# Strassen halves of an FFN cut inside each half of the tokens, a two-pass output projection and earlier fetches for the down products

## The chip, the cores and the metric

The kernel runs on one core of a Trainium2 chip. What counts is the device time of one launch in microseconds (us), as the median of several executions. A core has five engines that work side by side, each with its own queue of instructions: TensorE (PE, matrix products into PSUM), VectorE (DVE), ScalarE (ACT), GpSimd (POOL) and SyncE (SP, which here issues the DMAs). An instruction waits at the head of its queue until its operands and its buffer are there, and all that is queued behind it on that engine waits too.

## The reference, cut to what matters

Two layers work on 1032 tokens (1024 of a prompt, 8 of a sample group) with 1024 features each. Everything is float32.

```python
for l in range(DEPTH):                                    # DEPTH = 2
    main, mo = mixer(l, rmsnorm(x, norm_mix_g[l]))        # layer 0: RG-LRU, layer 1: windowed attention
    x = x + concat([main, mo]) @ w_out[l]                 # output projection, 1024 x 1024
    hn = rmsnorm(x, norm_ffn_g[l])
    u = hn @ w_ffn_up[l]                                  # 1024 x 6144: gates, values
    u = causal_dwconv(u, width=3) + bias
    x = x + (gelu(u[:, :3072]) * u[:, 3072:]) @ w_ffn_down[l]
```

The change touches three stages of each layer: the output projection, the up products and the start of the down products. The mixers stay as they are.

## The kernel before, in words

Features lie on the 128 partitions, tokens on the free axis. Nearly all data live in one pool of 44 row buffers of 128 x 1032 numbers (`row()`); small ones of 392 columns come from a pool of 12 (`sm()`), and products go to 8 PSUM buffers of 512 columns (`ps()`).

A product keeps float32 accuracy by splitting each operand into a high part (a rounded copy, made by ACT at L108) and a low part (the operand less the high part, a subtraction by DVE at L116 or by POOL at L119). `mm3` then makes three matmuls of each pair of tiles: L301 (high by high), L302 (high by low) and L303 (low by high). Helpers record most vector instructions, so one line stands for many: L108 is every activation or copy of ACT, L116 `vtt` and L122 `stt` on DVE (the second also scales by a gain), L119 `gtt` on POOL.

**Output projection** (`out_proj`). The tokens are cut into four quarters of 258 (QW). The eight output blocks are worked through in passes (layer 0: blocks 0 to 3, then 4 to 7; layer 1: 0 and 1, 2 and 3, then 4 to 7); within a pass it goes quarter by quarter, and in each quarter block by block. A tile is 24 matmuls of 258 columns; DVE then adds its PSUM to the residual `x[m]`. A weight is fetched and split once, and held through its pass. After each quarter of the last pass `on_block` starts the norm of this quarter.

**Norm and operands** (`enter_ffn`). `norm(q)` stores the quarter of the residual to DRAM (`rD`), squares and sums it, multiplies the sums by a matrix of ones on PE (L580), and scales the eight blocks with eight instructions on DVE (L122). The up products follow Strassen's scheme in Winograd's form: gates and values of block pair j, the two halves of the features, and the two halves of the tokens (columns 0 to 515 and 516 to 1031) make the 2 x 2 blocks. Seven products P1 to P7 stand for eight. Their token operands B11, B21, B22 and the differences T1 to T4 (28 tiles of 516 columns with a high and a low part each) are made once per layer. B22 and T1 to T4 need quarters 2 and 3 of the tokens, so they come after the last quarter's norm.

**Up products** (`ffn`). There are 24 pairs. Each product's weights are combined on POOL and split (copy by ACT, low part by POOL, 512 columns each) five products ahead (AHEAD). A product is 24 matmuls of 258 columns in two column halves, each in a PSUM buffer of its own. Pairs 0 and 1 are interleaved product by product (`ENTRY`); from pair 2 on the order is `STEADY`. After a pair, `post` runs the convolution (one activation, two taps on DVE at L122, an add for the sample tokens), gelu and the product, and stores the gated block to DRAM (`gD`, L883).

**Down products.** The 24 gated blocks are read in four chunks of six. For chunk 0 six blocks are loaded (L953) and split on ACT and DVE, then the eight tiles of the residual are loaded again from `rD` (L979), and the first weight of `w_ffn_down` is asked for (L254). A tile of the residual takes three PSUM buffers (384, 384 and 264 columns) per chunk.

**What sets the order.** ACT follows the order in which the program is written. The other engines' queues are ordered by the framework's scheduler, which weighs its own estimates of when operands are ready. SP's queue holds all these DMAs; a load waits there until a row buffer is free, a store until its data is ready. `get` fetches and splits weights in the order of one list (`spec_...`), one ahead; a fence keeps the down weights from being asked for before the first `get` of one.

## Time and profile before

| | |
|---|---|
| median of 3 runs | 2588.8 us (2584.58 to 2590.01) |
| the profiled execution, its own time | 2590.59 us |
| its span | 2588.8 us |
| busy share of the span | PE 90%, DVE 60%, POOL 53%, ACT 41% |
| mean granted clock of PE | 0.951 of full speed |

The span is what the profiler saw from first to last instruction; 1.8 us of the execution's time lie around it. A slice of the page's picture is a fortieth of the span, 64.7 us, and a digit is the busy share of the slice in tenths. Layer 0's output projection ends in the 8th slice, its up products in the 16th; for layer 1 these are the 28th and the 36th.

### The profile page before, as it was taken

How to read it: one execution, taken by the hardware profiler on the slowest of the kernel's cores; microseconds unless marked ns; L12 is line 12 of the kernel's file. 1: busy time of each engine (PE TensorE's matmuls, PEld its weight loads, DVE VectorE, ACT ScalarE, POOL GpSimd, SP SyncE). 2: the span in 40 equal slices, each digit the busy share in tenths (PEclk: the TensorE clock that was granted, in tenths of full speed). 3: DMA queues.
4: the chain of work that ended last, by engine and by line, in shares of the span. 5: the costliest groups of instructions: out<-in, count | busy, mean ns of one | idle time of the engine just before them, and what ended most of it. 6: DMA issues, size and time to landing. Idle time of an engine off the chain costs nothing.

```text
span 2588.8 us, 42624 instructions
## 1 busy us (share of the span) xinstructions
PE 2327.0 (90%) x16590; PEld 2247.7 (87%) x16590; DVE 1560.5 (60%) x2786; ACT 1050.6 (41%) x2181; POOL 1384.2 (53%) x1083
## 2 busy tenths in 40 slices
PE   7996888499999995999989987794999999959999
PEld 6886788399999995999977877794999999959999
DVE  6759974756666664332478789737566666643221
ACT  5665552344343443111365577513443434431110
POOL 2247651578888882222144456325788888822120
PEclk8998989799999997999989999897999999979999
DMA  4221151022222215322574543630222222153221
GB/s 163 90 68 46 51 179 59 2 74 74 83 89 76 74 58 212 109 88 76 177 265 132 181 169 118 175 130 5 74 74 81 84 82 75 58 210 105 92 73 65
DMA packets 140186, 265.24 MB, mean 102 GB/s; under 512 B 28288, under 2 KB 85200, under 8 KB 139984
## 3 DMA queue, kind: packets, MB, share of 16 engines
q1 hardware_dynamic: 139984, 262.52, 29.8%
q8 instruction: 130, 2.13, 0.3%
q14 instruction: 72, 0.59, 0.1%
HBM read 203.60 MB, written 58.87 MB: 101 GB/s over the span
## 4 chain that ended last, share of the span: by engine, by line
PE 67%; DVE 8%; issue 6%; POOL 3%; ACT 3%; DMA 3%; SPq 0%; POOLq 0%; DVEq 0%; ACTq 0%
PE ps L301 21%; PE ps L302 21%; PE ps L303 21%; POOL row L119 3%; ACT row L108 2%; DVE row L116 2%; DVE row L122 1%; DVE sm L116 1%; DMA row<-in_w_ffn_down 1%; DVE ty L116 1%; DVE ty L398 1%; DMA row<-rD 1%; ACT sm L108 0%; DMA row<-mD 0%; DVE row L1140 0%
## 5 line engine op out<-in xcount | busy, mean ns | idle before, releaser
L301 PE MATMUL ps<-row,row 128*128 128x258 f32 (+4 forms) x5032 | 1500.4, 302 | 109.9 <-ACT row L108 107.0
L119 POOL TENSOR_TENSOR row<-row,row 128x512 fp32r<-128x512 f32 (+10 forms) x714 | 1127.5, 1602 | 833.6 <-ACT row L108 447.8
L302 PE MATMUL ps<-row,row 128*128 128x258 f32 (+4 forms) x5032 | 1503.0, 301 | 32.1 <-DVE row L116 27.9
L303 PE MATMUL ps<-row,row 128*128 128x258 f32 (+4 forms) x5032 | 1471.2, 300 | 9.3 <-POOL row L119 9.3
L301 PEld LDWEIGHTS ps<-row,row 128*128 128x128 f32 x5032 | 956.9, 191 | 128.0 <-ACT row L108 116.7
L302 PEld LDWEIGHTS ps<-row,row 128*128 128x128 f32 x5032 | 960.8, 191 | 48.4 <-DVE row L116 32.8
L303 PEld LDWEIGHTS ps<-row,row 128*128 128x128 f32 x5032 | 944.5, 191 | 18.2 <-POOL row L119 10.7
L108 ACT ACTIVATE row<-row 128x512 fp32r<-128x512 f32 (+8 forms) x684 | 469.5, 723 | 987.4 <-POOL row L119 281.7
L116 DVE TENSOR_TENSOR row<-row,ps 128x258 f32<-128x258 f32 (+2 forms) x736 | 322.3, 445 | 746.8 <-PE ps L303 735.2
L122 DVE SCALAR_TENSOR_TENSOR row<-row,fw,row 128x1023 f32<-128x1023 f32 x192 | 272.1, 1436 | 64.2 <-ACT row L108 63.9
L116 DVE TENSOR_TENSOR row<-row,row 128x1032 f32<-128x1032 f32 (+8 forms) x220 | 222.0, 1027 | 56.8 <-ACT row L108 46.7
L108 ACT ACTIVATE row<-ps 128x258 f32<-128x258 f32 (+6 forms) x430 | 157.7, 407 | 97.6 <-PE ps L303 47.8
L119 POOL TENSOR_TENSOR row<-row,ty 128x768 f32<-128x768 f32 (+2 forms) x56 | 77.1, 1378 | 158.6 <-DVE ty L415 65.4
L108 ACT ACTIVATE row<-row,fw 128x1032 f32<-128x1032 f32 x96 | 114.9, 1244 | 66.1 <-DVE row L116 66.1
L116 DVE TENSOR_TENSOR row<-row,sb 128x8 f32<-128x8 f32 x96 | 105.5, 1099 | 0.0
L108 ACT ACTIVATE sm<-row 128x258 f32<-128x258 f32 (+3 forms) x130 | 51.1, 450 | 112.9 <-DVE row L122 57.9
L108 ACT ACTIVATE row<-ps,ty,ty 128x256 f32<-128x256 f32 (+1 forms) x160 | 87.5, 564 | 7.9 <-DVE ty L116 5.7
L116 DVE TENSOR_TENSOR sm<-sm,sm 128x258 f32<-128x258 f32 (+5 forms) x125 | 75.9, 616 | 19.6 <-ACT sm L108 15.9
L108 ACT ACTIVATE sm<-ps 128x384 f32<-128x384 f32 (+5 forms) x156 | 65.3, 445 | 38.3 <-PE ps L433 22.7
L116 DVE TENSOR_TENSOR row<-ps,row 128x384 fp32r<-128x384 f32 (+2 forms) x125 | 63.5, 519 | 23.2 <-ACT row L108 9.9
L119 POOL TENSOR_TENSOR row<-row 128x512 f32<-128x512 f32 x48 | 62.9, 1311 | 23.5 <-DMA rD<-row 16.1
L119 POOL TENSOR_TENSOR sm<-sm,row 128x192 f32<-128x192 f32 (+3 forms) x72 | 49.3, 698 | 36.1 <-ACT sm L108 18.6
(162 smaller groups left out, 1488.0 us busy)
## 6 DMA issues: line engine op xcount, KB each, us to landing
row<-in_w_ffn_up SPq DMA_DIRECT2D x96, 512.0 KB, 3.2
gD<-row SPq DMA_DIRECT2D x48, 516.0 KB, 2.6
row<-gD SPq DMA_DIRECT2D x48, 516.0 KB, 4.1
row<-in_w_ffn_down SPq DMA_DIRECT2D x64, 384.0 KB, 3.1
row<-hD SPq DMA_DIRECT2D x48, 512.0 KB, 6.5
rD<-row SPq DMA_DIRECT2D x64, 129.0 KB, 2.5
row<-rD SPq DMA_DIRECT2D x16, 516.0 KB, 9.9
row<-in_w_out SPq DMA_DIRECT2D x16, 512.0 KB, 4.7
```

Of the source, the lines that this page charges most:

```text
L108: return nc.scalar.activation(out, in_, func, **kw)
L116: return V.tensor_tensor(out=out, in0=a, in1=b, op=op)
L119: return G.tensor_tensor(out=out, in0=a, in1=b, op=op)
L122: return V.scalar_tensor_tensor(out=out, in0=a, scalar=s, in1=b, op0=op0, op1=op1)
L301: T.matmul(out, ah, bh, start=first and j == 0, stop=False, skip_group_check=more)
L302: T.matmul(out, ah, bl, start=False, stop=False, skip_group_check=more)
L303: T.matmul(out, al, bh, start=False, stop=last and j == n - 1, skip_group_check=more)
L398: V.tensor_reduce(out=mx[:, c0 : c0 + m], in_=s3, axis=AX.X, op=amax, negate=True)
```

## The change

**Strassen halves inside each token half.** Token half 0 is quarters 0 and 1, half 1 is quarters 2 and 3. The columns of a 2 x 2 scheme are now the two quarters of one half, so that each half has its own operands B11 to T4, with 258 columns each, in the same buffers. A product is the same 24 matmuls, 12 for each token half, with one PSUM buffer per half, and the result goes to the same places of the gates and values.

**Projection in two passes.** `out_proj` goes through all eight blocks for token half 0, then again for half 1; the weights stand twice in the list, so each is fetched and split twice. `on_tile` stores a quarter tile of the residual and squares and sums it as soon as it is added. `on_half` makes both sums' inverse roots (matmul with ones, now at L1334 of the new kernel) and starts the operands of this half. Norm and operands of half 0 and the seven combined weights of pair 0 (`first_pair`) are written beside the second pass. Pair 0 then runs first for half 0, then for half 1; pair 1 is no longer interleaved with it.

**Fetches in the last pair.** While the seven products of the last pair are issued, `fetch` loads gated blocks 0 to 5, `gated` splits blocks 0 to 4, and the first two down weights are asked for. The residual's tiles come two ahead of the tile in which they are needed (`refill`), and the blocks of the next chunk two before they are split.

Lines that only move, and removed lines that the code above shows, are left out:

```diff
 STEADY = ("P1", "P6", "P2", "P7", "P5", "P4", "P3")
-ENTRY = (
-    (0, "P1"), (1, "P1"), (0, "P2"), (1, "P2"), (0, "P6"), (1, "P6"), (0, "P7"), (1, "P7"), (0, "P4"), (1, "P4"),
-    (0, "P5"), (0, "P3"), (1, "P5"), (1, "P3"),
-)
-SEQUENCE = ENTRY + tuple((j, p) for j in range(2, KF) for p in STEADY)
+ENTRY = tuple((0, p, (0,)) for p in STEADY) + tuple((0, p, (1,)) for p in ("P1", "P2", "P6", "P7", "P5", "P4", "P3"))
+SEQUENCE = ENTRY + tuple((j, p, (0, 1)) for j in range(1, KF) for p in STEADY)
...
     def spec_out(l):
+        for hb in range(2):
+            for m in range(KD):
+                spec(f"out{l}.{hb}.{m}", I["w_out"][l, m, 0], (8, P))
...
+    def out_proj(l, mget, ks, x, on_tile, on_half):
+        for hb in range(2):
+            for m in range(KD):
+                key = f"out{l}.{hb}.{m}"
+                wh, wl = get(key, 1, 1)
+                if x[m] is None:
+                    x[m] = residual(l, m)
+                for q in (2 * hb, 2 * hb + 1):
+                    c0 = QB[q]
                     p = ps()
                     mm3(p[:, :QW], [(wh[:, k * P : k * P + P], wl[:, k * P : k * P + P]) + mget(k, c0, QW) for k in ks])
                     vtt(x[m][:, c0 : c0 + QW], x[m][:, c0 : c0 + QW], p[:, :QW], add)
+                    on_tile(q, m)
                     tick()
+                drop(key)
+            on_half(hb)
...
             if name == "P1":
-                load_pair(j + 1)
+                if j:
+                    load_pair(j + 1)
...
+        def product(j, name, hfs):
+            w = made[j, name]
+            if hfs[-1] == 1:
+                del made[j, name]
             group = {"P1": "X", "P2": "X", "P6": "Y", "P7": "Y", "P4": "Y", "P5": "Z", "P3": "Z"}[name]
             fresh = name in ("P1", "P6", "P5")
             B = PRODUCTS[name]
+            for hf in hfs:
+                if fresh:
+                    bank[j, group, hf] = ps()
                 terms = []
                 for kk in range(4):
+                    need(B, kk, hf)
+                    terms.append((w[:, kk * P : kk * P + P], w[:, 512 + kk * P : 512 + kk * P + P]) + ops[B, kk, hf])
+                mm3(bank[j, group, hf][:, :QW], terms, fresh, True, not fresh)
...
+        gh, gl, ga = {}, {}, {}
+        def fetch(j):
+            ga[j] = row()
+            SY.dma_start(ga[j][:, :NT], gD[l, j])
...
+        def refill(m):
+            x[m] = row()
+            SY.dma_start(x[m][:, :NT], rD[l, m])
         last = []
-        for q, (j, name) in enumerate(SEQUENCE):
-            while at < min(len(SEQUENCE), q + AHEAD):
-                combine(*SEQUENCE[at])
+        todo = [(0, p) for p in STEADY] + [(j, p) for j, p, _ in SEQUENCE if j]
+        at = 7
+        for q, (j, name, hfs) in enumerate(SEQUENCE):
+            if q == 6:
+                load_pair(1)
+            want = 7 if q < 10 else min(len(todo), q - 7 + AHEAD)
+            while at < want:
+                combine(*todo[at])
                 at += 1
-            t = product(j, name)
+            if j == KF - 1:
+                i = STEADY.index(name)
+                if i < DCH:
+                    fetch(i)
+                if i > 1:
+                    gated(i - 2)
+                if i == 4:
+                    get(f"dn{l}.0.0", 0, 1)
         def down(c, m, b):
...
-        for j in range(DCH):
+        for j in range(5, DCH):
             gated(j)
-            tick()
+        refill(0)
+        refill(1)
         for t in last:
             finish(t)
         SY.dma_start(O[4][l], ul)
-        for m in range(KD):
-            x[m] = row()
-            SY.dma_start(x[m][:, :NT], rD[l, m])
         for c in range(NDC - 1):
             for m in range(KD):
-                if m >= 2:
+                if c == 0 and m + 2 < KD:
+                    refill(m + 2)
+                if m < DCH:
+                    fetch((c + 1) * DCH + m)
+                if m > 1:
...
     def enter_ffn(l, x, mh, ml):
+        ops, gen, sums = {}, {}, {}
+        def split(name, kk, hf, pair, raw, on_pool):
             hi, lo = pair
             acopy(hi, raw)
             (gtt if on_pool else vtt)(lo, raw, f(hi), sub)
+            ops[name, kk, hf] = pair
+        def cols(q):
+            return slice(QB[q], QB[q] + QW)
+        def on_tile(q, m):
+            SY.dma_start(rD[l, m, :, cols(q)], x[m][:, cols(q)])
+            if m == 0:
+                sums[q] = sm()
+                act(sums[q][:, :QW], x[m][:, cols(q)], AF.Square)
+            else:
+                t = sm()
+                act(t[:, :QW], x[m][:, cols(q)], AF.Square)
+                vtt(sums[q][:, :QW], sums[q][:, :QW], t[:, :QW], add)
+        def inverse(q):
+            a = sums.pop(q)
+            p = ps()
+            T.matmul(p[:, :QW], ones, a[:, :QW], start=True, stop=True)
+            m, out, t = sm()[:, :QW], sm()[:, :QW], sm()[:, :QW]
+            ts(V, m, p[:, :QW], 1.0 / D, EPS, mul, add)
+            act(out, m, AF.Ln)
+            act(out, out, AF.Exp, scale=-0.5)
+            stt(t, m, -0.5, out, mul, mul)
+            vtt(t, t, out, mul)
+            stt(out, t, 1.5, out, add, mul)
+            return out
+        def norm(hf):
+            qa, qb = cols(2 * hf), cols(2 * hf + 1)
+            ra, rb = inverse(2 * hf), inverse(2 * hf + 1)
+            yield
+            xs = lambda k, part: x[k][:, part]
+            def scale(k, part, r):
+                stt(xs(k, part), xs(k, part), g_ffn[l][k], r, mul, mul)
+            def slot(k, part):
+                return mh[k][:, part], ml[k][:, part]
+            def own(n):
+                for i in range(n):
+                    if i % 2 == 0:
+                        t = row(F32R)
+                    b = (i % 2) * 2 * QW
+                    yield t[:, b : b + QW], t[:, b + QW : b + 2 * QW]
             for k in range(KD):
+                scale(k, qa, ra)
+                split("B11" if k < 4 else "B21", k % 4, hf, slot(k, qa), xs(k, qa), k % 2)
+                if k % 4 == 3:
                     yield
...
+            t2 = own(4)
+            for kk in range(4):
+                scale(kk, qb, rb)
+                scale(kk + 4, qb, rb)
+                vtt(xs(kk, qa), xs(kk, qb), xs(kk, qa), sub)
+                vtt(xs(kk, qb), xs(kk + 4, qb), xs(kk, qb), sub)
+                split("B22", kk, hf, slot(kk + 4, qb), xs(kk + 4, qb), True)
+                vtt(xs(kk + 4, qb), xs(kk + 4, qb), xs(kk, qa), sub)
+                split("T2", kk, hf, next(t2), xs(kk + 4, qb), False)
+                if kk % 2:
                     yield
+            t2 = own(4)
+            for kk in range(4):
+                split("T3", kk, hf, next(t2), xs(kk, qb), kk % 2)
+            yield
+            for kk in range(4):
+                split("T1", kk, hf, slot(kk, qb), xs(kk, qa), kk % 2)
+                if hf:
                     x[kk] = None
+            yield
+            t2 = own(4)
+            for kk in range(4):
+                vtt(xs(kk + 4, qa), xs(kk + 4, qa), xs(kk + 4, qb), sub)
+                split("T4", kk, hf, next(t2), xs(kk + 4, qa), kk % 2)
+                if hf:
                     x[kk + 4] = None
+            yield
+        weights = up_weights(l)
+        def first_pair():
+            weights[0](0)
+            yield
+            yield
+            yield
+            for name in STEADY:
+                weights[1](0, name)
+                yield
+        def on_half(hf):
+            if hf:
+                finish(gen["w"])
+            gen[hf] = start(norm(hf))
+            if not hf:
+                gen["w"] = spawn(first_pair())
+        def need(name, kk, hf):
+            while (name, kk, hf) not in ops:
+                advance(gen[hf])
+        return on_tile, on_half, need, ops, weights
...
```

**First place: SP's queue from the last up products of layer 0 to its first down products.** gD are the stored gated blocks, rD the stored residual, ul a small output. Of the kernel before, then of the changed one:

```order
L953 DMA row_10369<-gD 128x1032
L979 DMA row_10376<-rD 128x1032
L979 DMA row_10378<-rD 128x1032
L979 DMA row_10380<-rD 128x1032
L979 DMA row_10382<-rD 128x1032
L979 DMA row_10384<-rD 128x1032
L979 DMA row_10386<-rD 128x1032
L979 DMA row_10388<-rD 128x1032
L979 DMA row_10390<-rD 128x1032
L254 DMA row_10392<-in_w_ffn_down 128x768
L254 DMA row_10398<-in_w_ffn_down 128x768
```

```order
L941 DMA row_10274<-gD 128x1032
L941 DMA row_10310<-gD 128x1032
L941 DMA row_10342<-gD 128x1032
L888 DMA gD<-row_10229 128x1032
L941 DMA row_10374<-gD 128x1032
L941 DMA row_10408<-gD 128x1032
L251 DMA row_10414<-in_w_ffn_down 128x768
L251 DMA row_10420<-in_w_ffn_down 128x768
L941 DMA row_10448<-gD 128x1032
L995 DMA out<-ul 128x480
L951 DMA row_10497<-rD 128x1032
L951 DMA row_10499<-rD 128x1032
```

Before, the last two of the six gated blocks and the eight residual tiles stood ahead of the first down weight; now the gated blocks come first, weights 1 and 2 behind the fifth of them, and the residual after them, two tiles at first.

**Second place: DVE near the end of layer 0's output projection.** An add with ps is the residual add of a tile; an instruction with pack scales by the gain; sm are sums and roots of the norm. Before, then after:

```order
L122 SCALAR_TENSOR_TENSOR sm_4262<-sm_4498,sm_4262 128x258
L116 TENSOR_TENSOR row_4043<-row_4043,ps_4472 128x258
L116 TENSOR_TENSOR sm_4425<-sm_4425,sm_4504 128x258
L122 SCALAR_TENSOR_TENSOR row_3489<-row_3489,pack,sm_4262 128x258
L122 SCALAR_TENSOR_TENSOR row_3530<-row_3530,pack,sm_4262 128x258
L122 SCALAR_TENSOR_TENSOR row_3573<-row_3573,pack,sm_4262 128x258
L122 SCALAR_TENSOR_TENSOR row_3611<-row_3611,pack,sm_4262 128x258
L122 SCALAR_TENSOR_TENSOR row_3977<-row_3977,pack,sm_4262 128x258
L122 SCALAR_TENSOR_TENSOR row_4011<-row_4011,pack,sm_4262 128x258
L122 SCALAR_TENSOR_TENSOR row_4043<-row_4043,pack,sm_4262 128x258
L122 SCALAR_TENSOR_TENSOR row_4071<-row_4071,pack,sm_4262 128x258
L116 TENSOR_TENSOR sm_4425<-sm_4425,sm_4507 128x258
L116 TENSOR_TENSOR row_4071<-row_4071,ps_4510 128x258
```

```order
L119 SCALAR_TENSOR_TENSOR sm_4068<-sm_4069,sm_4068 128x258
L119 SCALAR_TENSOR_TENSOR row_3489<-row_3489,pack,sm_4068 128x258
L119 SCALAR_TENSOR_TENSOR row_3595<-row_3595,pack,sm_4068 128x258
L119 SCALAR_TENSOR_TENSOR sm_4081<-sm_4079,sm_4080 128x258
L119 SCALAR_TENSOR_TENSOR row_3663<-row_3663,pack,sm_4068 128x258
L119 SCALAR_TENSOR_TENSOR row_3731<-row_3731,pack,sm_4068 128x258
L119 SCALAR_TENSOR_TENSOR row_3799<-row_3799,pack,sm_4068 128x258
L119 SCALAR_TENSOR_TENSOR row_3867<-row_3867,pack,sm_4068 128x258
L119 SCALAR_TENSOR_TENSOR row_3935<-row_3935,pack,sm_4068 128x258
L119 SCALAR_TENSOR_TENSOR row_4003<-row_4003,pack,sm_4068 128x258
L113 TENSOR_TENSOR sm_4081<-sm_4081,sm_4080 128x258
L113 TENSOR_TENSOR row_3489<-row_3489,ps_4094 128x258
```

Before, these were the scalings of one quarter and the adds of the last tiles. Now this is the start of the second pass, and the add of its first tile (row_3489 with ps_4094) stands behind the root and the scalings of half 0.

**Third place: PE at the end of layer 0's output projection.** ps_4510 before is the PSUM of the projection's last tile, L301 to L303 are the three matmuls of `mm3` (L298 to L300 in the changed kernel). Before, then after:

```order
L303 MATMUL ps_4510<-row_3475,row_4040 128x258
L301 MATMUL ps_4510<-row_3479,row_4039 128x258
L302 MATMUL ps_4510<-row_3480,row_4039 128x258
L303 MATMUL ps_4510<-row_3479,row_4040 128x258
L301 MATMUL ps_4573<-row_3459,row_4551 128x258
L301 MATMUL ps_4574<-row_3459,row_4551 128x258
L301 MATMUL ps_4642<-row_3459,row_4558 128x258
L301 MATMUL ps_4643<-row_3459,row_4558 128x258
L302 MATMUL ps_4573<-row_3460,row_4551 128x258
L303 MATMUL ps_4573<-row_3459,row_4551 128x258
```

```order
L298 MATMUL ps_4700<-row_3479,row_4606 128x258
L299 MATMUL ps_4700<-row_3480,row_4606 128x258
L300 MATMUL ps_4700<-row_3479,row_4607 128x258
L1334 MATMUL ps_4730<-sm_4121,ones 128x258
L1334 MATMUL ps_4741<-sm_4166,ones 128x258
L298 MATMUL ps_4754<-row_3459,row_4284 128x258
L299 MATMUL ps_4754<-row_3460,row_4284 128x258
L300 MATMUL ps_4754<-row_3459,row_4284 128x258
```

Before, the products of pairs 0 and 1 followed the last tile, and the ones matmul of the last quarters stood further behind. Now the two ones matmuls stand at once behind the last tile, and the products of pair 0 for half 0 after them.

## Rows read from the trace of the kernel before

**Rows 1.** The page: busy time of each engine, and PE in 40 slices.

```profile
PE 2327.0 (90%) x16590; PEld 2247.7 (87%) x16590; DVE 1560.5 (60%) x2786; ACT 1050.6 (41%) x2181; POOL 1384.2 (53%) x1083
...
PE   7996888499999995999989987794999999959999
```

**Rows 2.** Waits of PE: waiter <- releaser: us idle, count, longest wait.

```profile
PE ps L301 <- ACT row L108: 107.0, 20, 31.2
```

**Rows 3.** Stretches: us, busy PE, PEld, DVE, ACT, POOL, clock, DMA share, GB/s.

```profile
984.00:1016.00 32.00, 0.77 (x5) 0.56 (x4) 13.66 (x14) 10.68 (x11) 0.55 (x2) 0.57 0.79 291
1016.00:1018.00 2.00, 2.00 (x7) 1.87 (x7) 0.00 (x0) 1.35 (x2) 2.00 (x2) 0.50 1.04 422
1018.00:1020.00 2.00, 2.00 (x10) 2.00 (x10) 0.00 (x0) 1.19 (x2) 2.00 (x2) 0.72 1.02 412
1030.00:1290.00 260.00, 260.00 (x1650) 259.31 (x1649) 84.80 (x140) 55.89 (x85) 55.56 (x30) 1.00 0.34 109
2280.00:2311.00 31.00, 0.52 (x4) 0.31 (x3) 13.64 (x14) 10.52 (x11) 0.40 (x2) 0.59 0.76 290
```

**Rows 4.** Chain that ended last, layer 0's seam: start us, us, what.

```profile
996.99 7.75 DMA row<-rD
...
1004.80 9.85 DMA row<-in_w_ffn_down
```

**Rows 5.** Stretches of the entry of both layers, columns as in rows 3.

```profile
360.00:443.00 83.00, 83.00 (x692) 82.89 (x691) 36.79 (x72) 19.04 (x45) 19.11 (x12) 1.00 0.41 142
443.00:516.00 73.00, 31.71 (x188) 27.62 (x186) 57.43 (x75) 26.01 (x56) 46.22 (x29) 0.74 0.03 12
1660.00:1700.00 40.00, 39.33 (x309) 38.98 (x308) 19.99 (x47) 13.82 (x27) 15.27 (x10) 0.95 0.92 277
1751.00:1813.00 62.00, 28.04 (x170) 24.14 (x169) 45.62 (x69) 23.91 (x52) 38.07 (x23) 0.78 0.01 3
```

**Rows 6.** Groups, 984 to 1016 us: busy us, mean ns | idle before, releaser.

```profile
L116 DVE TENSOR_TENSOR row<-row,row 128x1032 fp32r<-128x1032 f32 x6 | 7.3, 1230 | 6.3 <-ACT row L108 6.3
L122 DVE SCALAR_TENSOR_TENSOR row<-row,fw,row 128x1023 f32<-128x1023 f32 x2 | 2.6, 1281 | 1.4 <-ACT row L108 1.4
L108 ACT ACTIVATE row<-row,fw 128x1032 f32<-128x1032 f32 x2 | 2.4, 1239 | 9.0 <-DVE row L116 9.0
L116 DVE TENSOR_TENSOR row<-row,sb 128x8 f32<-128x8 f32 x2 | 0.3, 166 | 0.0
```

**Rows 7.** Groups, 359 to 480 us, layer 0's entry, columns as in rows 6.

```profile
L119 POOL TENSOR_TENSOR row<-row,row 128x1024 fp32r<-128x1024 f32 x5 | 12.2, 2456 | 4.5 <-ACT row L108 4.5
L119 POOL TENSOR_TENSOR row<-row,row 128x264 fp32r<-128x264 f32 x4 | 3.7, 946 | 0.0
L116 DVE TENSOR_TENSOR row<-row,ps 128x258 f32<-128x258 f32 x31 | 12.9, 421 | 39.9 <-PE ps L303 39.3 <-DMA row<-in_x_t 0.5
L108 ACT ACTIVATE sm<-row 128x258 f32<-128x258 f32 x32 | 11.1, 411 | 28.3 <-DVE row L116 28.3
```

**Rows 8.** Timeline of layer 0's entry: start us, us, instructions xcount [idle before].

```profile
431.17 0.42 DVE L116 TENSOR_TENSOR sm<-sm,sm 128x258 f32<-128x258 f32 x1
431.51 1.68 DVE L122 SCALAR_TENSOR_TENSOR row<-row,pack,sm 128x258 f32<-128x258 f32 x4
447.72 5.71 DVE L122 SCALAR_TENSOR_TENSOR row<-row,pack,sm 128x258 f32<-128x258 f32 x4
448.89 4.25 POOL L119 TENSOR_TENSOR row<-row,row 128x512 fp32r<-128x512 f32 x3
483.72 1.23 PE L580 MATMUL ps<-sm,ones 128*128 128x258 f32 x2 [9.17 <-DVE sm L116]
490.57 6.43 POOL L119 TENSOR_TENSOR row<-row,row 128x516 fp32r<-128x516 f32 x1 [11.89 <-ACT row L108]
```

## What the change is predicted to do, before its result was known

> **What bounds the kernel now.** I read the page first: TensorE (PE) is busy 90% of the span, and its row of 40 slices stands at 8 or 9 except in a few [rows 1]. The four low slices after the opening are of interest here: the 8th and the 28th, where output projection passes into the FFN, and the 16th and the 36th, where the FFN's up products pass into the down products. So this is a PE-bound kernel with four holes, two per layer. Next I read who PE waited for: the dearest entry by far is the first matmul of a triple waiting for a ScalarE copy, 107 us in 20 waits [rows 2]. Then I cut the span into stages around the holes.
>
> The **seam** (up to down): PE works 0.8 us of 32 in layer 0 and 0.5 of 31 in layer 1, that is 31.2 and 30.5 us idle [rows 3]. The clock restarts at 0.50 and 0.72 in the two stretches of 2 us behind it, which costs 1.0 + 0.56 = 1.6 us in layer 0; I take the same in layer 1. Meanwhile the DMAs run at a share of 0.79, and the chain of waits names them: the reload of the residual, then the first down weights, 9.85 us [rows 4]. The weights stand last in the queue.
>
> The **entry** (projection to up): in layer 0 PE works 31.7 of the 73 us from 443 to 516, in layer 1 28.0 of the 62 from 1751 to 1813: 41.3 and 34.0 us idle [rows 5]. Here the DMAs are at a share of 0.03 and 0.01; what is late is the norm and the operand sums on VectorE (DVE), ScalarE (ACT) and GpSimd (POOL). Before the entry PE runs without a break: 692 matmuls in 83 us, 0.12 us each [rows 5].
>
> **The seam, after.** The change puts gated blocks 0 to 5 and the first two weights ahead of the residual on SP's queue (first place of the order), so the DMAs fall beside 7 products of the last pair. Count from the last up matmul. Still late are gated blocks 4 and 5: on DVE their low parts stand behind the last pair's convolution. ACT: a convolution start 1.24 us. DVE: three taps of 1.28 us, the low part of block 4 (1.23), one more tap, the low part of block 5 (1.23) [rows 6]. With about 1.8 us until the first tap can start, that is 1.8 + 3.8 + 0.2 (two small edge adds) + 1.2 = 7.0 us for block 4 and 9.5 for block 5. PE has 36 matmuls for blocks 0 to 3 in the meantime, 0.158 us each (260 us by 1650 in [rows 3]): 5.7 us; then 9 for block 4, 1.4 us. It stops at 5.7 for 1.3 us and at 8.4 for 1.1. I add 1.5 us because the low parts of blocks 0 to 2 (1.23 each) now sit between the PSUM reads of the last pair. That gives 4 us in place of 31: if the copies hide wholly it is 2, if the fetches come late it is 10. The clock should not fall in pauses this short. Gain: 61.7 + 3.2 - 8 = 57 us for both layers (45 to 62). The residual now comes two tiles ahead; its first use waits, but 8 PSUM buffers at three per weight tile carry PE past it, some 20 us.
>
> **The entry, after.** The arithmetic of PE is the same: 32 projection tiles, then 24 matmuls per product, only now in two halves of 12. What moves is when the vector work stands. The whole norm of tokens half 0 (scaling, differences, 28 splits) and the seven combined weights of pair 0 now lie beside the second half of the projection, which also splits its eight weights a second time. PE needs 16 x 24 x 0.12 = 46.1 us there. What must fit beside it:
>
> POOL has 32 instructions by the order: 7 of 1024 columns at 2.46 us [rows 7], 11 of 512 at 1.42 (4.25 by 3 in [rows 8]), 14 of 258. For the last there is no row: 264 columns took 0.95 beside a busy DVE [rows 7], half of the 512 is 0.71; I take 0.75. Sum 17.2 + 15.6 + 10.5 = 43.3 us.
>
> DVE has 83, of which 18 read PSUM (0.42 us, the same whether POOL works or not [rows 7]) and 65 have both inputs in SBUF. These are the point. Alone, four scalings take 1.68 us; with POOL working, four take 5.71, and POOL does one instruction per 1.42 us in that time [rows 8]: DVE gets one through for each of POOL's. So 32 of the 65 go in POOL's shadow and 33 need time of their own, 33 x 0.42 = 13.9 us. 43.3 + 13.9 = 57.2 us. Both queues also wait: SP issues the projection weights behind the stores of the residual, which wait for DVE, where the residual add stands behind 15 scalings (second place of the order). I add 5 us, so 62 against 46: PE loses 16 us in this half. Bounds: POOL alone, with the last weight's two tiles behind it, 43.3 + 5.8 = 49, a loss of 3; with everything one after the other, 43.3 + 65 x 0.42 = 70.6, a loss of 24.
>
> The Trainium skill speaks for the far end: "SBUF — State Buffer", section "Who interferes with whom", says that a DVE instruction with both inputs in SBUF and a GpSimd instruction that reads SBUF hold a shared port pair as an exclusive lock, the second blocked for the whole instruction. That agrees with the 5.71 against 1.68 us, and with the POOL instruction of 6.43 us that stood while DVE streamed [rows 8]. By the rule alone both times add up to 70.6 us and the sum of this forecast would be 16 us later, 2541. I stay with 62, since in the rows POOL kept its pace while one DVE instruction went by.
>
> Each half ends in a matmul with ones that PE now meets at once in its queue (third place of the order): residual add 0.42, square 0.41, sum 0.42 [rows 7, 8], the matmul itself 0.6 (two in 1.23 us [rows 8]): 2 us, twice per layer, 4 us. Now this wait lies inside the holes counted above.
>
> Then pair 0, half 1. Behind the second ones matmul DVE has 51 SBUF instructions and 8 PSUM reads up to the release of the second T3 product: 51 x 0.42 + 8 x 0.42 = 24.8 us, and POOL's 14 splits of 0.75, each hiding one of DVE's: + 14 x 0.33 = 4.6. 29.4 us. PE has 12 half products beside it, 144 matmuls, 17.3 us. Loss 12 us (6 if DVE's tail isn't on the path, 20 if POOL's weights of pair 1 come late too). These are ready about when PE gets there: POOL's pair takes 11 instructions.
>
> One us for the first half, whose weights come twice as fast. In layer 1 its DMAs ask for 8 x (512 + 512 + 258) KB, 10.5 MB in 46 us or 228 GB/s; the chip gave 277 GB/s at a share of 0.92 in that stage and PE lost 0.7 us of 40 [rows 5], so I cost it at nothing, at 5 us if the reads of 512 bytes go slower. Sum 16 + 4 + 12 + 1 = 33 us per layer against 41.3 and 34.0: a gain of 8 and of 1, less 1 for layer 1's DMA: 8 us in all (38 gained to 38 lost by the bounds). The cold clock behind pauses I take as before.
>
> **Sum.** The profiled execution took 2590.6 us (span 2588.8, 1.8 around it); less 57 and 8 is 2525.6. That execution lies 1.8 us over the median of the runs shown, so 2524 to 2525: I say 2525.
>
> **Rivals.**
> 1. The vector work of half 0 really hides: inputs that come late leave POOL idle while DVE runs, and the two overlap to the low bounds, 3 + 4 + 6 + 1 = 14 us per layer. 2525 - 38 = 2487. For it: POOL is idle 64 of the 83 us before the entry now [rows 5]. Against: the order gives POOL nothing to do early, the 32 instructions all fall in the second half. 18%.
> 2. The seam closes only in part: the gated blocks need free row buffers and SP holds three of them behind the store of pair 22. If they come with the last product, six of 516 KB at 290 GB/s [rows 3] take 11 us, plus copies: 16 us per seam. 2525 + 24 = 2549. Against: the last pair has no next pair to load, so buffers come free early. 15%.
> 3. DVE and POOL fully one after the other: losses 24 + 4 + 20 + 1 = 49 us per layer, 2525 + 32 = 2557. For it the 6.43 us wait, against it the steady 1.42 [rows 8]. 16%.
> 4. Slower than before. One mechanism: every SBUF instruction of DVE pays a whole POOL instruction, 1.43 us, in both stretches. 65 x 1.43 = 93 us in the projection half, a loss of 47; 51 x 1.43 + 3.4 - 17.3 = 59 in pair 0; with 5, 111 us per layer, 2525 + 156 = 2681. It decides from 33 + 32 = 65 us of entry loss per layer. For it: from 447.72 on it was so for four in a row [rows 8]. Against: POOL has 32 and 14 instructions to pay with, not 65 and 51. 6%.
>
> **How the numbers follow.** The forecast 2525 has 45%, its own range 2508 to 2545. Rivals 1, 2 and 3 have 18, 15 and 16%, and all are faster; rival 4 has 6%. The range reaches from just above rival 1's end to past rival 3's, 2494 to 2565. A measurement of this kernel can tell about 0.2%, 5 us, from no change. Faster 0.92; within 0.2%, a mixture of 3 and 4, 0.02; slower 0.06.
>
> **What would show it.** Right: the two seams with under 10 us of PE idle each, and the clock at 1.00 behind them; the residual reloads spread over the first down tiles. In the second half of the projection DVE busy nearly throughout, its SBUF instructions at 1 us or more in the mean, and PE losing 10 to 20 us in stretches that end with ACT, DVE or POOL of a projection weight; behind the second ones matmul PE waiting for low parts and PSUM reads, 8 to 16 us. The steady pairs at 0.12 us per matmul as now. Wrong: a seam over 15 us (rival 2), a projection half of under 52 us (rival 1) or over 70 (rival 3 or 4), or new idle time in the pairs from 2 on, where I expect none.

## The result and the profile after

The changed kernel takes 2544.7 us (median, 2541.5 to 2545.8), the kernel before 2589.4 in the same comparison: a ratio of 0.983, 95% interval 0.981 to 0.985. That is 45 us faster where 64 were forecast. The forecast 2525 is 20 us too low, inside its range of 2494 to 2565.

The page after: the slices in which the up products pass into the down products are full now, those of the entries are not [rows 1].

```profile
PE 2339.4 (92%) x16590; PEld 2255.1 (89%) x16590; DVE 1582.0 (62%) x2850; ACT 1075.7 (42%) x2253; POOL 1419.4 (56%) x1123
...
PE   7996877799999999999988988787999999999999
```

PE does as many matmuls, 16,590, and is busy 12 us longer, 2339 against 2327: time in which it is busy and slow. To see where, I cut both traces at the same matmuls, counted from the first one of a layer's projection (mixers, rounding and the last three chunks make up the rest of the 45 us):

| us | layer 0 before | after | layer 1 before | after |
|---|---|---|---|---|
| projection, first half of its matmuls | 58.0 | 79.2 | 60.6 | 65.4 |
| projection, second half | 49.1 | 75.5 | 47.1 | 68.5 |
| pairs 0 and 1 | 92.4 | 55.7 | 84.0 | 55.8 |
| pair 2 | 21.4 | 20.6 | 21.3 | 20.4 |
| last pair, to the first down matmul | 51.5 | 24.4 | 50.8 | 23.8 |
| first chunk of the down products | 69.8 | 70.9 | 70.8 | 70.9 |

The two seams give 27.1 + 27.0 us, less 1.1 and 0.1 in the chunk behind them: 53 us. The entry costs 10 us in layer 0 and gives 3 in layer 1: 7 us lost where 8 were to be gained.

Here are the windows of the seams after (columns as in [rows 3]; they answer to its 984:1016 and 2280:2311): the last matmuls of pair 23 and the first of the down products in layer 0, then the former in layer 1. PE is idle 2.5, 2.4 and 1.9 us where it was idle 31.

```profile
989.40:999.30 9.90, 7.41 (x50) 7.37 (x50) 6.66 (x10) 2.01 (x3) 3.03 (x3) 0.83 0.67 239
999.30:1012.00 12.70, 10.34 (x65) 9.86 (x64) 10.38 (x14) 7.91 (x8) 5.00 (x3) 1.00 0.87 314
...
2256.00:2265.50 9.50, 7.58 (x51) 7.40 (x50) 6.20 (x10) 1.80 (x2) 2.65 (x3) 0.82 0.65 241
```

The entries, cut as in the table: first half, second half, pairs 0 and 1 of layer 0, then of layer 1. Before:

```profile
340.25:398.29 58.04, 51.39 (x386) 49.78 (x385) 33.62 (x50) 17.07 (x34) 29.68 (x16) 0.89 0.61 209
398.29:447.34 49.05, 47.08 (x390) 46.76 (x388) 22.43 (x51) 12.91 (x32) 5.43 (x4) 1.00 0.20 66
447.34:539.77 92.43, 51.33 (x340) 47.45 (x341) 62.84 (x90) 32.06 (x62) 62.23 (x44) 0.78 0.04 13
1643.56:1704.17 60.61, 55.10 (x424) 53.97 (x422) 29.10 (x76) 22.49 (x47) 22.89 (x16) 0.94 0.85 254
1704.17:1751.27 47.10, 47.06 (x390) 46.74 (x389) 21.06 (x54) 9.31 (x27) 7.04 (x6) 1.00 0.14 46
1751.27:1835.30 84.03, 50.06 (x341) 46.37 (x341) 54.89 (x88) 32.06 (x62) 56.77 (x38) 0.82 0.04 15
```

And after:

```profile
341.10:420.27 79.17, 56.35 (x389) 53.14 (x389) 32.41 (x63) 23.55 (x48) 30.29 (x17) 0.82 0.45 143
420.27:495.76 75.49, 57.00 (x391) 55.35 (x389) 50.48 (x85) 28.20 (x64) 43.74 (x32) 0.82 0.26 83
495.76:551.47 55.71, 47.30 (x338) 43.91 (x337) 41.55 (x79) 23.51 (x53) 33.49 (x33) 0.91 0.19 67
1627.96:1693.33 65.37, 56.65 (x429) 53.77 (x427) 44.65 (x96) 28.74 (x60) 25.37 (x15) 0.94 0.82 244
1693.33:1761.80 68.47, 52.72 (x391) 51.27 (x389) 42.70 (x84) 26.86 (x60) 40.44 (x30) 0.88 0.19 62
1761.80:1817.58 55.78, 47.47 (x338) 44.11 (x337) 41.02 (x79) 23.52 (x53) 33.74 (x33) 0.91 0.20 67
```

A row splits in two: length less PE's busy time is idle; busy time less 0.12 us per matmul (384, 384 and 336 of them) is what PE lost while it worked, called slow work here (in layer 1's first half some 40 matmuls of the mixer are in it too, before and after). Summed over the three rows, layer 0 is idle 49.7 us before and after, and its slow work grows from 17.3 to 28.2 us. In layer 1 idle time falls from 39.5 to 32.8, slow work rises from 19.7 to 24.4. So the idle time moved by 7 us in all where the sum had 8, but by luck: the sum had the 8 in layer 0, where nothing came, and nothing in layer 1, where 7 came. The slow work took 15.6 us that the sum did not have. By the trace's record of the granted clock PE was busy at 0.50 for 65.6 us in these six rows, before for 39.5; at 0.21 us a matmul instead of 0.12 this difference is some 11 of the 15.6 us (an estimate); the rest is open.

### The profile page after: what moved, and what is told of

Its sections match the earlier page's. It is cut to its first block, busy times and chain, and to the rows that moved or that the text cites. A ratio compares the mean times of both kernels' runs of the same rounds, so it can differ in the third digit from the quotient of the medians.

```text
span 2544.0 us, 42855 instructions
## 1 busy us (share of the span) xinstructions
PE 2339.4 (92%) x16590; PEld 2255.1 (89%) x16590; DVE 1582.0 (62%) x2850; ACT 1075.7 (42%) x2253; POOL 1419.4 (56%) x1123
## 4 chain that ended last, share of the span: by engine, by line
PE 64%; DVE 8%; issue 2%; ACT 2%; DMA 2%; POOL 1%; SPq 0%; POOLq 0%; ACTq 0%; DVEq 0%
PE ps L299 21%; PE ps L298 21%; PE ps L300 21%; DVE row L113 2%; ACT row L105 1%; DVE sm L113 1%; DVE row L119 1%; POOL row L116 1%; DVE ty L113 1%; DVE ty L396 1%; DMA row<-in_w_out 1%; DVE ty L119 0%; DMA row<-mD 0%; ACT sm L105 0%; PE ps L422 0%
## 5 line engine op out<-in xcount | busy, mean ns | idle before, releaser
L116 POOL TENSOR_TENSOR row<-row,row 128x512 fp32r<-128x512 f32 (+9 forms) x754 | 1164.6, 1566 | 789.4 <-ACT row L105 472.8
L298 PE MATMUL ps<-row,row 128*128 128x258 f32 (+4 forms) x5032 | 1511.9, 303 | 54.5 <-ACT row L105 44.4
L300 PE MATMUL ps<-row,row 128*128 128x258 f32 (+4 forms) x5032 | 1471.0, 301 | 20.5 <-POOL row L116 20.5
L298 PEld LDWEIGHTS ps<-row,row 128*128 128x128 f32 x5032 | 963.7, 192 | 73.1 <-ACT row L105 49.8
L299 PEld LDWEIGHTS ps<-row,row 128*128 128x128 f32 x5032 | 965.1, 192 | 43.7 <-DVE row L113 24.1
L300 PEld LDWEIGHTS ps<-row,row 128*128 128x128 f32 x5032 | 948.4, 192 | 30.9 <-POOL row L116 23.4
L105 ACT ACTIVATE row<-row 128x512 fp32r<-128x512 f32 (+8 forms) x756 | 492.8, 690 | 922.5 <-POOL row L116 303.3
L119 DVE SCALAR_TENSOR_TENSOR row<-row,fw,row 128x1023 f32<-128x1023 f32 x192 | 264.7, 1397 | 67.3 <-ACT row L105 67.3
L113 DVE TENSOR_TENSOR row<-row,row 128x258 fp32r<-128x258 f32 (+7 forms) x268 | 242.9, 930 | 29.8 <-ACT row L105 15.8
L105 ACT ACTIVATE row<-ps 128x258 f32<-128x258 f32 (+6 forms) x430 | 157.3, 406 | 65.4 <-PE ps L300 26.1
L105 ACT ACTIVATE sm<-row 128x258 f32<-128x258 f32 (+3 forms) x130 | 54.6, 452 | 192.4 <-DVE row L113 129.4
L113 DVE TENSOR_TENSOR row<-row,sb 128x8 f32<-128x8 f32 x96 | 112.3, 1169 | 0.0
```

What stands on the lines that cost most here:

```text
L105: return nc.scalar.activation(out, in_, func, **kw)
L113: return V.tensor_tensor(out=out, in0=a, in1=b, op=op)
L116: return G.tensor_tensor(out=out, in0=a, in1=b, op=op)
L119: return V.scalar_tensor_tensor(out=out, in0=a, scalar=s, in1=b, op0=op0, op1=op1)
L298: T.matmul(out, ah, bh, start=first and j == 0, stop=False, skip_group_check=more)
L299: T.matmul(out, ah, bl, start=False, stop=False, skip_group_check=more)
```

## The experiments

Every run stands beside runs of the kernel before on the same chip. Medians of one kernel differ by some 3 us between jobs, so stages are read from the traces; a ratio is to the kernel before.

**seam_only.** The kernel before with the fetches of the last pair and the residual two tiles ahead:

```diff
+            if j == KF - 1:
+                i = STEADY.index(name)
+                if i < DCH:
+                    fetch(i)
+                if i > 1:
+                    gated(i - 2)
+                if i == 4:
+                    get(f"dn{l}.0.0", 0, 1)
...
-        for m in range(KD):
-            x[m] = row()
-            SY.dma_start(x[m][:, :NT], rD[l, m])
...
+                if c == 0 and m + 2 < KD:
+                    refill(m + 2)
...
```

> Only the last pair's fetches (gated blocks 0 to 5, two down weights, residual two tiles ahead); projection and entry as before. Theory A (from the two traces, stage by stage: the seam gained 27 us per layer, the entry lost 10 in layer 0 and gained 3 in layer 1): 2589 - 54 = 2535 us, faster than the whole change, with 24 us from pair 22's end to the first down matmul. Theory B (the entry gained 8 us as the forecast's sum had it, so the seam is worth only 45 - 8 = 37): 2552 us.

2536.6 us, ratio 0.979 (0.978 to 0.981); 24.4 and 24.3 us from pair 22 to the first down matmul. Theory A: the seam is the gain, and alone it is at least as fast as the whole change.

**seam_weights_late.** seam_only without the early `get`:

```diff
-                if i == 4:
-                    get(f"dn{l}.0.0", 0, 1)
```

> The kernel with the seam alone, but without asking for the first two down weights in the last pair: they stand behind three residual tiles and a gated block again. Theory A (each fetch that stands behind the residual shows in full): 4 x 516 KB at 290 GB/s are 7 us, with the weight and its split 12 us per seam, 2537 + 24 = 2561 us. Theory B (the gated blocks alone were the seam; two or three residual tiles are short enough to hide beside the last pair's convolution): 2537 to 2542 us.

2559.2 us, 0.989 (0.987 to 0.990); 36.3 and 35.7 us. In its chain of waits at layer 0's seam (start us, us, what) four issues of SP (three residual tiles, L949, and a gated block, L939) stand ahead of the weight's load:

```profile
989.46 0.38 SPq L949
...
990.44 0.38 SPq L949
...
990.91 0.38 SPq L939
...
991.35 7.72 DMA row<-in_w_ffn_down
...
999.15 0.85 ACT row L108
```

Theory A. Two weights of 384 KB, asked for early, are worth 23 of the seam's 53 us.

**entry_only.** The whole change with the last pair and the down products as before.

> Only the halves and the two-pass projection; from the last pair on as before. Theory A: the entry as a whole costs, 2589 + 8 = 2597 us; the first projection half of layer 0 takes 79 us and the second 75, as in the whole change. Theory B (entry gains 8): 2581 us.

```diff
-            if j == KF - 1:
-                i = STEADY.index(name)
...
-        for j in range(5, DCH):
+        for j in range(DCH):
             gated(j)
...
```

2592.9 us, 1.0016 (1.0007 to 1.0025): halves of 79.0 and 74.5 us in layer 0, 64.7 and 67.6 in layer 1. A little slower, by less than A had it; a gain of 8 is excluded. That is some 4 us, where the stages of the whole change gave 7; medians that differ by 3 us between jobs do not tell these apart.

**residual_early.** In layer 0's first half the trace after shows a ring. In its timeline (start us, us, instruction, [idle before <- releaser]) the add waits for the residual's load (`in_x_t`), SP's stores wait for the add, and the next load stands behind the stores: 7.1 us a block, while PE has 5.8 us of work. The next weight's load (`in_w_out`) stands behind the same stores, and in these blocks PE waits about 1 us for the weight's low part on POOL.

```profile
381.74 0.76 DVE L113 TENSOR_TENSOR row<-row,ps 128x258 f32<-128x258 f32 x2 [5.73 <-DMA row<-in_x_t]
...
382.19 0.80 SPq L1322 DMA_DIRECT2D rD<-row  x2
383.09 0.41 SPq L251 DMA_DIRECT2D row<-in_w_out  x1
383.55 0.45 SPq L772 DMA_DIRECT2D row<-in_x_t  x1
...
388.82 0.76 DVE L113 TENSOR_TENSOR row<-row,ps 128x258 f32<-128x258 f32 x2 [5.40 <-DMA row<-in_x_t]
389.27 0.80 SPq L1322 DMA_DIRECT2D rD<-row  x2
```

```diff
+                if not l and not hb and m + 1 < KD:
+                    x[m + 1] = residual(l, m + 1)
                 for q in (2 * hb, 2 * hb + 1):
```

> The whole change, with one difference: in layer 0's first pass the residual of block m + 1 is asked for before the stores of block m instead of behind them. Theory A (SyncE's queue is a closed loop there: load of the residual 5.3 us, add, store, next load; 7.15 us per block against 5.8 of TensorE work): the first half falls from 79 to about 60 us, 2545 - 19 = 2526 us. Theory B (the bytes of weight plus residual, 1 MB per block, or ScalarE's and GpSimd's split of the weight set the pace): no change, 2545 us.

2533.0 us, 0.978 (0.976 to 0.979). The first half falls from 79.2 to 67.3, not to 60:

```profile
337.69:405.03 67.34, 53.96 (x390) 51.73 (x389) 36.57 (x63) 23.71 (x48) 30.48 (x17) 0.85 0.52 167
```

The ring is shown, and is worth 12 of the 21 us. Of PE's idle time in this half 9.4 us go, most of it in the pauses of about 1 us per block and in the one before the ones matmul at its end (5.6 us, now 1.1).

**norm_spread, split_ahead, one_combination** try the second half. The first writes half 0's operands in 14 pieces:

```diff
-                if k % 4 == 3:
+                if k % 4 == 3 or not hf and k % 2:
                     yield
...
-                if kk % 2:
+                if kk % 2 or not hf:
                     yield
...
```

> The whole change, with the operands of token half 0 written in 14 pieces instead of 7, so that ScalarE meets a projection weight's copy after one block of operands instead of two. Theory A (latency: ScalarE's queue holds the weight's copy behind a chain from DVE to ScalarE to GpSimd and back, and the work is crowded into the first ten of the 16 tiles): second half from 75 and 68 to about 58 and 55 us, 2545 - 30 = 2515 us. Theory B (throughput: the summed vector work of DVE and GpSimd on their shared way to SBUF is 62 us or more wherever it stands): the second half stays at 65 to 75 us, 2535 to 2545 us.

2536.2 us, 0.980 (0.978 to 0.981); second halves 69.6 and 61.9 us (75.5 and 68.5). Of the 30 us that A forecast, 12 came in these halves, and 8 in the whole time.

```diff
-                wh, wl = get(key, 1, 1)
+                wh, wl = get(key, 1 + hb, 1)
```

> The whole change; in the second pass a projection weight is fetched and split two blocks ahead instead of one, so its copy stands a block earlier in ScalarE's queue. Nothing of the vector work changes. Theory A (TensorE waits because the weight's copy stands in ScalarE's queue behind operands of half 0 that wait for DVE and GpSimd): second half from 75 and 68 to about 60 and 57 us, 2545 - 25 = 2520 us. Theory B (the summed vector work is too long for the half): the second half stays within 3 us, 2540 to 2545 us.

2539.3 us, 0.980 (0.979 to 0.982); second halves 72.7 and 64.3. Theory A falls as the main cause: a block more of lead buys 3 and 4 us.

```diff
+            if j == 0 and name != "P1":
+                made[j, name] = made[j, "P1"]
...
+                return
             w = row(F32R)
...
```

> The whole change, but pair 0 uses the combined weight of P1 for all seven products: left out are six combined weights per layer, that is ten instructions on GpSimd (10 x 1.42 = 14 us) and six copies on ScalarE. Theory A (waits in ScalarE's queue): the second half falls by less than 6 us per layer, 2533 to 2545 us. Theory B (GpSimd's and DVE's work is too long): it falls by the 14 us, 2545 - 28 = 2517 us.

2528.3 us, 0.976 (0.975 to 0.978); second halves 67.3 and 62.5. This kernel leaves out six of pair 0's seven combined weights. The 14 us of POOL's work taken out, and six copies on ACT with them, give 8 and 6 us: at or above what A allows, about half of B. So neither ACT's queue alone nor the plain sum of POOL's and DVE's work explains the stretch.

**act_by_scheduler.**

```diff
+    act_in_order(False)
     out_proj(0, mgetA, ks_a, x, ot, oh)
+    act_in_order(True)
```

> The whole change; in layer 0's projection the framework's scheduler orders ScalarE instead of the order in which the program is written (in layer 1 it already does). Theory A (the hand-written order is why layer 0's second half takes 75 us and layer 1's 68): layer 0's second half falls to about 68, the first half stays at 79 because of the residual's load; 2545 - 7 = 2538 us. Theory B (the layers differ by something else, the DMAs for instance): second half at 75, 2545 us.

2528.3 us, 0.976 (0.974 to 0.978). Layer 0's halves, both against what I expected:

```profile
336.84:399.07 62.23, 51.88 (x389) 49.93 (x389) 43.02 (x63) 25.54 (x49) 37.23 (x19) 0.89 0.67 214
399.07:470.24 71.17, 51.95 (x391) 50.79 (x389) 44.89 (x84) 32.11 (x65) 40.53 (x30) 0.86 0.19 60
```

The second half gains only 4 us, and pairs 0 and 1 behind it lose as much (59.8 against 55.7), so ACT's order is a small part there. (In layer 1's mixer and projection the scheduler orders ACT in all these kernels; the rule that ACT follows the program holds for the rest.) The first half gains 17: DVE's adds wait for PE there again (at most 2.2 us from 362 to 392), no longer for the residual's load, so the ring is gone a second way. The trace is of an execution of 2520.4 us, 8 under the median.

**three_edits** joins early residual, 14 pieces and the longer lead.

> The whole change with the early residual of layer 0, the 14 pieces and the weight two blocks ahead together. Theory A: first half of layer 0 at 67 us as in the run with the early residual alone, second halves at about 56: 2545 - 12 - 19 - 12 = 2502 us. Theory B (vector work sums): second halves stay at 62 to 70, 2525 to 2530 us.

2517.1 us, 0.972 (0.970 to 0.973); first half of layer 0 66.9, second halves 66.5 and 54.6. A in layer 1, B in layer 0. Layer 1's first half rose from 65.4 to 71.1. The trace shows where: PE waits 8.0 and 3.1 us for the sums at the two ones matmuls that end this half, against 3.6 and 0.9 in the whole change. Why the sums come later there is open.

**four_edits.** After the first tile of layer 0 in the trace after, ACT stood 11.5 us at a square whose add had to wait for the residual, with token operands behind it, and PE waited 5.8 us for ACT:

```profile
357.83 0.42 ACT L105 ACTIVATE sm<-row 128x258 f32<-128x258 f32 x1 [11.48 <-DVE row L113]
...
358.72 0.58 PE L298 MATMUL ps<-row,row 128*128 128x258 f32 x1 [5.77 <-ACT row L105]
```

```diff
+            late.append((q, m))
+            while len(late) > 2:
+                square(*late.pop(0))
...
```

> As the kernel with three edits, and besides each square of the residual is written two tiles later on ScalarE and the residual is asked for a block early in layer 1 too. Theory A (ScalarE stands at a square that waits for its tile's add, with token operands and weight copies behind it: 345.9 to 357.8 us in the trace of the whole change): another 6 us in layer 0's first half and 3 in layer 1's, 2493 us. Theory B (the squares' place is of no consequence): as three edits.

2506.6 us, 0.968 (0.966 to 0.969), the fastest here, 1.5% under the whole change and 3.2% under the kernel before. Rows of layer 0's halves:

```profile
335.40:394.85 59.45, 52.49 (x389) 50.76 (x389) 43.78 (x63) 23.36 (x48) 33.13 (x17) 0.89 0.59 189
394.85:464.78 69.93, 54.54 (x390) 51.95 (x389) 56.99 (x85) 28.37 (x65) 44.08 (x32) 0.88 0.29 93
```

Beside the later squares it asks early for layer 1's residual too. Theory A for the first half: 59.5 us, 1.4 over the kernel before. It is a chain of two causes, then: the ring, and squares that hold up ACT. The total gains 10.5 us on three edits where A had 9; that it is 13 over A's 2493 is the shortfall of the three edits.

**six_edits** adds the scheduler's order in layer 0 and half 0's sums a block later (`on_half(0)` after the first block of the second pass).

```diff
-            on_half(hb)
+                if hb and not m:
+                    on_half(0)
+        on_half(1)
```

> The kernel with four edits, with layer 0's ScalarE ordered by the scheduler in the projection, and with the sums' matmul and the norm of half 0 one block later, so that TensorE has 48 matmuls to do while the last squares are summed. Theory A: layer 0's second half from 70 to about 56 as in layer 1 (14 us), the pauses at the sums (1 us in layer 0, 7 in layer 1, and the slow clock behind them) go: 2506 - 14 - 9 = 2483 us. Theory B (vector work is too long; what the block's delay gives at the sums it takes at the end of the half): 2500 to 2507 us.

2509.4 us, 0.969 (0.968 to 0.971): no gain on four edits; layer 0's second half 67.6, layer 1's 62.7. Layer 1's first half falls from 68.2 to 59.3 and its second rises by 7, so what the block's delay gives at the sums it takes later. Theory B.

**pauses_filled.**

```diff
+                if j == 0 and hf and name != "P1":
...
+                    if name == "P2":
+                        bank["fill"] = ps()
+                    for _ in range(7):
...
```

> The kernel with four edits; in pair 0 for token half 1, six times seven matmuls whose result nobody reads stand ahead of the products, where TensorE pauses about 1 us each (42 x 0.12 = 5 us of extra matmuls per layer). Theory A (the pauses themselves cost 7 to 8 us per layer, but the clock at 0.50 that follows costs another 6 to 9, and it falls because TensorE pauses): the clock stays at 1.00 there and pair 0 falls from 36 and 35 to 31 or 32 us, 2506.6 - 8 = 2499 us. Theory B (the stage ends when the last operand comes, whatever the clock): 35 to 37 us per layer as before, 2507 to 2512 us.

2513.8 us, 0.971 (0.970 to 0.973), and pair 0 takes 36.9 and 37.1 us (36.1 and 35.0 with four edits): not faster, with 10 us of fillers, matmuls whose result nobody reads. Theory B by the time, but it does not settle the clock's part: most fillers ran early in the stage, the later pauses stayed (2.2, 1.0 and 1.0 us in layer 0), and the clock still stood at 0.50 behind them.

## Why the prediction was right, and where it was not

- **The seam: right.** The gain is 53 us, forecast 57; seam_only alone gives 53. In the first down matmuls PE pauses twice, 2.4 us where the sum had 1.3 + 1.1, but only the first pause is the sum's: the low part of block 4 lets PE go on 7.1 us after the first down matmul, where 7.0 us behind the up products were forecast, and the pause before it is 0.8 us. Block 5 comes in time. The second pause is for the low part of the second down weight, which POOL made in 4.28 us beside a busy DVE (1.84 for the first weight's); the sum had no such term, and that the two add up to 2.4 is luck. Mis-sized is the term of 1.5 us for the low parts on DVE between the last pair's PSUM reads: a pair takes 20.1 us, so of 24.4 and 23.8 it cost 4.3 and 3.7, with a pause of 2.5 us in layer 0. The first line here is that pause, the others the two in the first down matmuls:

```profile
991.96 0.36 PE L298 MATMUL ps<-row,row 128*128 128x258 f32 x1 [2.49 <-DVE row L113]
...
1006.37 0.44 PE L299 MATMUL ps<-row,row 128*128 128x384 f32 x1 [0.80 <-DVE row L113]
...
1011.53 0.44 PE L300 MATMUL ps<-row,row 128*128 128x384 f32 x1 [1.56 <-POOL row L116]
```

- **"The clock should not fall in pauses this short": wrong.** With that pause the granted clock is 0.83 in the mean of the window above, and the window's 50 matmuls take 7.4 us (at 0.12 us 6.0). So nearly all of the 3.2 us of slow clock that the two seams were to give back went into the last pairs instead.
- **"The cold clock behind pauses I take as before": by the sum's terms the step that failed.** Slow work in the entries is 52.6 us against 37.0 before (28.2 + 24.4, 17.3 + 19.7): 15.6 of the 20 us by which the forecast missed, some 11 of them at the lower clock by the estimate above. Before, three pauses held most of layer 0's idle time (9.9, 13.5 and the 9.2 of [rows 8]); now it lies in many shorter ones, and slow work follows most of them. Windows around layer 0's second half and in pair 0 after; the third column from the right is the clock, 1.00 for 2.4 GHz and 0.50 for 1.2:

```profile
418.00:420.00 2.00, 1.25 (x3) 1.06 (x4) 0.84 (x3) 1.86 (x3) 0.00 (x0) 0.50 0.52 151
420.00:422.00 2.00, 2.00 (x9) 1.81 (x9) 0.99 (x3) 0.84 (x2) 0.00 (x0) 0.50 0.93 307
...
451.00:455.00 4.00, 1.51 (x5) 1.22 (x6) 2.97 (x3) 2.23 (x6) 4.00 (x3) 0.50 0.00 0
455.00:460.00 5.00, 5.00 (x24) 5.00 (x25) 1.52 (x2) 1.25 (x4) 4.92 (x5) 0.50 0.00 0
...
469.00:472.00 3.00, 3.00 (x15) 3.00 (x15) 0.38 (x1) 0.00 (x0) 3.00 (x4) 0.50 0.52 175
475.00:490.00 15.00, 15.00 (x128) 15.00 (x127) 6.20 (x11) 5.47 (x10) 7.33 (x4) 1.00 0.29 89
...
505.00:515.00 10.00, 5.19 (x35) 4.16 (x33) 9.30 (x27) 1.16 (x4) 1.62 (x2) 1.00 0.14 54
515.00:522.50 7.50, 4.89 (x12) 3.18 (x13) 5.83 (x12) 4.89 (x16) 3.76 (x6) 0.51 0.00 0
```

  From 455 to 460 PE is busy all the time and does 24 matmuls; from 475 to 490 it does 128 in 15 us. That the clock is what the pauses cost twice is read from these rows; the one run made to change it did not, and its time came out as its Theory B had it. So it is not shown that these stages would be shorter at the full clock: a stage whose length DVE and POOL set would have idle time of PE in place of the slow work.
- **"One us for the first half": wrong in layer 0**, 22.8 us idle against 6.7 before. I had counted the weights' bytes in layer 1 and found them hidden, which was so (8.7 us idle against 5.5); in layer 0 the residual's load stood in SP's queue behind stores that wait for DVE, and ACT stood at a square (5.8 us of PE's wait). I had named that queue for the second half and priced it there at 5. Of the 22.8 us, 5.6 are the wait at the ones matmul, a term of 2 us in the sum; over both halves this term was 4 us per layer and measured 6.6 and 5.5.
- **The second half: idle time about right, length not.** Forecast were 16 us lost in a half of 62; idle are 18.5 and 15.8, but with slow work the halves take 75.5 and 68.5. In layer 0 that is over the 70 that I had named as a sign of being wrong. POOL's work was as counted (32 instructions, 43.7 us busy against 43.3), and DVE's SBUF instructions took 0.7 us in the mean, less than the 1 us I had looked for. POOL was idle for 32 of the 75 us and DVE for 25, but seldom together: in layer 0 one of the two or both work for 65.9 us and neither for 9.6, in layer 1 for 60.4 and 8.0. The sum had 57.2 and 5, so both of its terms are too small. Of POOL's 32 us idle 26 ended with ACT, of DVE's 25 us 17 with a tile of PE: the engines waited for one another. Three runs each took away a part (pieces, lead, POOL's work) and each gave some 3 to 8 us. What the remaining 70 us in layer 0 wait for, where layer 1 comes to 55, stays open; ACT's order is not the answer (71.2 against 75.5). With four edits PE waits 12 us there for copies and low parts of weights on ACT and POOL, in layer 1's second half 3.5; but layer 1's first half is 8.7 us longer than layer 0's, so the two halves together differ by 5 us only (129.4 and 124.1).
- **DVE and POOL** do hold each other up: in layer 1's second half one POOL instruction of 512 columns took 4.74 us while DVE ran eleven without a break, as below; it ended 1.1 us after the last of them, and in layer 0's second half such an instruction takes 1.3 us in the mean. This agrees with the Trainium skill ("SBUF — State Buffer", "Who interferes with whom"), by which the two lock each other out of a shared port pair. The sum by that rule is still no floor: with three edits layer 1's second half has 65 SBUF instructions of DVE and 27 of POOL, 27.3 and 32.1 us at the prediction's prices, and takes 54.6 us, not 59.4.

```profile
1716.93 4.74 POOL L116 TENSOR_TENSOR row<-row,row 128x512 fp32r<-128x512 f32 x1 [4.09 <-ACT row L105]
...
1716.75 0.75 DVE L113 TENSOR_TENSOR row<-row 128x258 f32<-128x258 f32 x2
1717.43 0.41 DVE L113 TENSOR_TENSOR row<-row,row 128x258 fp32r<-128x258 f32 x1
1717.77 0.42 DVE L113 TENSOR_TENSOR row<-row 128x258 f32<-128x258 f32 x1
1718.10 0.75 DVE L113 TENSOR_TENSOR row<-row,row 128x258 fp32r<-128x258 f32 x2
1718.78 0.42 DVE L113 TENSOR_TENSOR row<-row 128x258 f32<-128x258 f32 x1
1719.12 0.42 DVE L113 TENSOR_TENSOR sm<-sm,sm 128x258 f32<-128x258 f32 x1
1719.45 1.09 DVE L113 TENSOR_TENSOR row<-row,row 128x258 fp32r<-128x258 f32 x3
```

- **Pair 0: right in sum, partly by luck.** 12 us were forecast. Pairs 0 and 1 take 15.4 and 15.5 us more than the 40.3 of their matmuls; of this 8.4 and 8.3 are idle time, less than forecast, and slow work makes up the rest.
- **The rivals.** 2 and 3 ended near the result (2549, 2557). 2 is not what happened: the seam closed, if with little to spare. SP did stand 11.9 us at the fetches of gated blocks (from 969.4) and issued the down weights at 988.8, and the first one's low part was ready at 998.0, 1.3 us before the first down matmul. 3 is partly what happened: it gave a half of 70.6 us, and DVE or POOL worked for 65.9 and 60.4 us, between it and the forecast; but they do overlap, as the run with three edits shows above. 1 fails, since the entry does not hide. 4 fails: it needed 1.43 us for each of DVE's SBUF instructions, and they took 0.7 in the mean.
- **Two slips in the sums** that change nothing here: the seam's gain has the upper bound 61 by its own terms, not 62, and of the entry's bounds the 38 gained is a distance from the forecast (14 us lost per layer in place of 33), while no sum given there comes to 38 lost (rival 3 gives 32).

## What to carry to other kernels

A wait is priced with its pauses counted: in layer 0's entry 49.7 us of idle time cost 17.3 us of slow work when three pauses held most of it, and 28.2 when it lay in many. When a load is moved, look in its queue for stores ahead of it and follow what they wait for; a ring through another engine sets a pace that no busy share shows. And ask of a change with two parts what each is worth alone: here the seam gave all of the gain, and the entry paid only after its stores, squares and pieces had been moved too.

## What was not expected of the hardware

Matmuls of 258 columns take about 0.21 us each (24 in 5.00 us, with the granted clock at 0.50) behind pauses of 4.9 and 1.7 us in the rows above, against 0.12 at 1.00. In layer 0's first half, where PE paused about 1 us per block, it stayed at 1.00 (the row below); in pair 0, with pauses of 0.8 to 1.6 us between the products, it fell (0.51 from 515 to 522.5, above):

```profile
385.00:410.00 25.00, 20.67 (x165) 19.92 (x164) 4.57 (x12) 5.11 (x9) 8.57 (x4) 1.00 0.59 199
```
